# The first 512 sigmoid-gate columns of a decoder block, from four whole projections to seven half-sized products with three weight sums kept in HBM

## The chip, the cores and the metric

One core of one Trainium2 chip runs the whole block. The metric is the device time of one execution in microseconds; three executions of the kernel before gave 772.45, 772.70 and 772.75 us, so its median is 772.7 us. All tensors are float32. The matrix engine takes every factor as two parts, a high part `h` (rounded) and a low part `l = t - h`, and forms `h*h + h*l + l*h`; so each weight tile that is loaded costs one copy on the scalar engine and one subtraction on the vector engine before it can be used, and each product costs three matmuls where one would do.

Engine names below are those of the profile: PE (matrix engine), PEld (its weight loads), DVE (vector), ACT (scalar), POOL, SP (issues most DMAs).

## What is computed

One layer (DEPTH = 1) on 512 tokens of width 1024, cut to what this change touches:

```python
h = rms_norm(x, norm_mix)                       # 512 x 1024
proj = h @ w_in                                 # w_in: 1024 x 4400
u, q, kc, vc, ksl, vsl, kwn, vwn, g_nsa, g_merge = split(proj)
y_pool = pool_mixer(u, w_pool, pool_scale)      # 512 x 512
y_nsa  = nsa_mixer(q, kc, vc, ...)              # 512 x 1024, 16 heads, three branches
g_a, g_b = split(sigmoid(g_merge))              # 2 x 1024 columns
merged = g_a * (y_pool @ w_proj_pool) + g_b * (y_nsa @ w_proj_nsa)
x = x + merged @ w_out
x = x + square(relu(rms_norm(x) @ w_ff1)) @ w_ff2
return rms_norm(x, norm_final)
```

The change concerns `g_a`: 1024 columns of `w_in` (columns 2352 to 3375), in two groups of 512, here called group 0 and group 1.

## The kernel before

**Stages.** The program runs in four stretches on one core: a first stretch of projections out of `h` (in the profile about 11 to 166 us), attention with the remaining projections as filler between its small matmuls (to about 376 us), the output projections (to about 453 us), and the MLP. The first stretch is written as one list of keys, `P1`; each key is a weight tile and a piece of PE work. `ck`, `cv`, `ks`, `kw` are key and value projections, `u0` to `u3` the pooling inputs, `q0` to `q2` the first query pairs, `wk*` and `wv*` the first layer of the compression MLP for keys and values, `V0` to `V2` the value projection in three slices of the contraction, `wpool` and `PO0` to `PO3` the pooling mixer's output matmuls, `pp*` the pool projection. `ga0` to `ga3` are the four 128-column tiles of gate group 0.

**A projection** (`fm`, line 683; `mms`, line 519) is 24 matmuls of 512 columns (8 slices of the contraction, three part products each) into one PSUM bank.

**A half-sized group** (`class Group`, `product`, line 589). Gate group 1 is already formed with seven products instead of eight (Strassen's scheme in Winograd's form). The weights of a group, 1024 x 512, are cut into quarters `A11`, `A12`, `A21`, `A22`, each 512 x 256; `h` is cut into quarters 11, 12, 21, 22 (half the contraction by half the tokens). `S1` to `S4` are sums of weight quarters (`S1 = A21+A22`, `S3 = A11+A21`, `S2 = S1+A11`, `S4 = A12+S2`; signs are kept on the other side), `T1` to `T4` sums and differences of the quarters of `h`. The products are `A11*11`, `S3*T3`, `S1*T1`, `S2*T2`, `A12*21`, `A22*T4`, `S4*22`; each is 24 matmuls of 256 columns. They fill four PSUM banks: a (`A11`, then `A12` on top), b (`S2`), c (`S3`, then `A22` on top), d (`S1`, then `S4` on top). Before a bank is added to, DVE has to have read what stood in it: `main` copies a on ACT, and DVE forms `u2 = a - b`, `u3 = c + u2`, `u3 = d + u3` (lines 610, 611, 614); `last` forms the remaining results (line 624) and ACT applies the sigmoid (line 1123). So `A22`'s matmuls wait both for `T4` and for DVE's read of bank c.

**The token sums** `T1` to `T4` (`token_sums`, lines 1088 to 1107) are made once, on DVE and ACT, out of `h`. `T4` lies where the compression MLP for values keeps its intermediate results, so its two halves (ACT line 1104, DVE line 1107) come after that MLP's last small matmul (line 992), which in turn needs transposes (line 964), an ACT copy (`cg`, line 967) and the four `wv` matmuls (line 930).

**Loads and splits.** SP issues the weight loads in list order (`emit_load`, line 277) into four buffers `raw`; a load can be issued when the buffer it takes has been split. The split writes `wh`/`wl`, two pairs of buffers in turn (line 475 ACT and 478 DVE in halves; line 405 ACT and 407 DVE whole, for gate quarters), or the one pair `wkt`, used by `wk*`, `wv*` and by the products `S1` and `A22`. Sums of quarters of gate group 1 are formed in the `raw` buffers by DVE (line 403).

**Sums in HBM.** For the output projection and the MLP, sums of weight quarters are made without any engine's arithmetic: SP copies one quarter from HBM to HBM (`make_sum`, line 311) and, when that has landed, POOL adds the other quarter with an accumulating DMA (`add_sum`, line 319). `jobs` is the list of these sums; `sums_after(i)` says after which load one is begun, `begun` holds those whose addition is still to be issued. A copy whose source is itself such a sum waits on SP for the addition.

**Order.** Every engine runs its instructions in the order in which the program lists them. A small scheduler sets that order from the order of emission (generators in `side`, stepped once per piece of PE work) and a few marks of priority.

Of the kernel before, what the change touches and what calls it, by code (L numbers as in the profile page):

```python
# [62 lines left out]
def trunk(ctx: ExitStack, tc: tile.TileContext, A, out):  # L63
# [54 lines left out]
    def add_key(k):  # L118
# [14 lines left out]
        else:  # L133
# [1 line left out]
            add_cols(k, w_in, c0 + 128 * i)  # L135

    IN_COLS = {"ck": 1536, "cv": 1664, "ks": 1792, "kw": 2048}
    P1 = ("ck ks u0 wk0 u1 wk1 u2 wk2 kw wk3 cv V0 V1 V2 wv0 "
          "u3 wv1 q0 wv2 wpool ga0 PO0 ga1 q1 PO1 wv3 ga2 ga3 A11G1 PO2 S3G1 S1G1 S2G1 PO3 A12G1 "
          "A22G1 S4G1 q2 pp0 pp1 pp2 pp3").split()  # L140
    FILL2 = "gb0 q3 q4 q5 gb1 gb2 q6 gb3 q7 gb4 gb5 gb6 gb7".split()
    IN_TURN = ("A11", "S3", "S1", "S2", "A12", "A22", "S4")
    gate_loads = {}

    def add_gates(g):

        at = {b: len(LD) + n for n, b in enumerate(("21", "11", "22", "12"))}
        for b in at:
            i, j, c = int(b[0]) - 1, int(b[1]) - 1, 2352 + 512 * g
            w = w_in[512 * j:512 * j + 512, c + 256 * i:c + 256 * i + 256]  # L150
            LD.append([(w.rearrange("(k p) c -> p k c", p=128), 0)])
        gate_loads[g] = at

    for k in P1 + FILL2:
        if k[-2] == "G":
            if k[:3] == "A11":
                add_gates(int(k[-1]))
            WL.append((k, None))
        elif k[:2] != "PO":
            add_key(k)  # L160
        if k == P1[-1]:
            N1 = len(LD)
# [4 lines left out]
    WO_LATE = {"A22": 2, "S4": 3}  # L167
    WO_TURN = ("A11", "S1", "S3", "S2", "A12", "A22", "S4")
    wo_at = {}
    dp = ctx.enter_context(tc.tile_pool(name="sums", bufs=1, space=bass.MemoryType.DRAM))  # L170
    jobs, late, later = [], [], []
    wo_of = {f"A{i + 1}{j + 1}": w_o[512 * j:512 * j + 512, 256 * i:256 * i + 256].rearrange("(k p) c -> p k c", p=128)
             for i in range(2) for j in range(2)}
    for o, x, y in (("S1", "A21", "A22"), ("S3", "A11", "A21"), ("S2", "S1", "A11")):
# [83 lines left out]
    def emit_load():  # L258

        i = st["load"]  # L260
        if i >= len(LD):
            return False
        segs = LD[i]
        a = segs[0][0].shape[1]
        b = sum(s.shape[2] for s, _ in segs)
        assert a * b <= 1024
        if not by_name() or st["kept"] < RAW:
            st["kept"] += by_name()
            t = wp.tile([128, 1024], F32, tag="raw", bufs=RAW, name=f"raw{i}")
        elif spare:  # L270
            t = spare.pop(0)
        else:
            return False
        st["load"] += 1
        v = t[:, :a * b].rearrange("p (a b) -> p a b", a=a)
        for s, o in segs:
            began[0] = nc.sync.dma_start(v[:, :, o:o + s.shape[2]], s)
        raws[i] = (t, a, b)
        for _ in range(sums_after(i)):
            make_sum(began[0])  # L280
        if (26 <= i < N1 and len(begun) > 1) or i >= N1 + len(FILL2) + 4 and (len(begun) > 2 or begun and st["sums"] == len(jobs)):
            add_sum()
        while i == MLP0 + 6 and len(begun) > 2:
            add_sum()
        return True

    def sums_after(i):

        if i < MLP0:
            return 26 <= i < N1 and i % 2 == 0 or N1 + 3 <= i < N1 + len(FILL2) or i == MLP0 - 2  # L290
        if i < MLP0 + 12:
            return {3: 1, 6: 4}.get(i - MLP0, 0)
        return i % 3 == 0
# [35 lines left out]
    def slot_of(i):  # L329

        return shifted(slot_tiles(i), WL[i][0])
# [50 lines left out]
            held[to] = t  # L382

    kept = {}

    def gate_steps(i):

        o, g = WL[i][0][:-2], int(WL[i][0][-1])
        if o == "A11":
            kept.clear()  # L390
        for b in {"A11": ("11",), "S3": ("21",), "S1": ("22",), "A12": ("12",)}.get(o, ()):
            while st["load"] <= gate_loads[g][b]:
                assert emit_load()
# [1631 lines left out]
```

## Time and profile before

| | |
|---|---|
| median of three executions | 772.7 us |
| the profiled execution: its time, its span from first to last instruction | 773.65 us, 771.9 us |
| TensorE clock granted | 0.997 |
| busy: PE, PEld, DVE, ACT, POOL | 759.2, 674.9, 657.6, 507.9, 179.5 us |
| first stretch, 28.20 to 166.20 us: PE busy | 137.76 of 138.00 us |
| HBM read, written | 140.97 MB, 51.38 MB |

The profiled execution's span is 1.75 us under its own time, and its time 0.95 us over the median. Matmuls overlap: the profile gives one 512-column matmul a mean of some 0.39 us, but 24 of them follow each other in about 5.46 us; what a stretch of matmuls costs is read from start to start. A busy PE in this profile can hide waits of a tenth of a microsecond.

### The profile page before, as it was taken

The page shows a single profiled execution, that of the slowest core. Times are in us where ns is not written, and L with a number is a line of the kernel's source. Part 1 is how long each engine was busy: PE and PEld are TensorE (multiplying, and loading weights), DVE is VectorE, ACT ScalarE, POOL GpSimd, SP SyncE. Part 2 cuts the span into 40 slices and gives each one's busy share as a digit, 9 for nine tenths or more (in the row PEclk, how much of TensorE's full clock was granted, in tenths as well). Part 3 has the DMA queues.
Part 4 walks back from the last instruction along what each step waited for, and adds up shares of the span by engine and source line. Part 5 has one row for each costly group of instructions (what it writes and reads, how often), then busy time and mean ns, then how long its engine had stood idle before and what let it go on. Part 6 is the DMA issues. An engine that isn't in the chain of part 4 may idle for free.

```text
span 771.9 us, 13216 instructions
## 1 busy us (share of the span) xinstructions
PE 759.2 (98%) x4675; PEld 674.9 (87%) x4675; DVE 657.6 (85%) x1267; ACT 507.9 (66%) x977; POOL 179.5 (23%) x261
## 2 busy tenths in 40 slices
PE   8999999999999999999999999999999999999996
PEld 6889889888888888888889899989998899889985
DVE  6899868467988989989689679997899789978997
ACT  6668546247978888899645566953774477447754
POOL 4000011116646766574000110101111111111101
PEclk9999999999999999999999999999999999999998
DMA  9554875984051923281357975989997999899952
GB/s 304 144 146 121 231 170 156 213 217 124 15 147 56 183 55 70 48 144 48 120 180 222 327 117 177 288 210 269 320 279 209 301 316 250 229 316 296 279 189 109
DMA packets 117708, 146.55 MB, mean 190 GB/s; under 512 B 5653, under 2 KB 90169, under 8 KB 117434
## 3 DMA queue, kind: packets, MB, share of 16 engines
q1 hardware_dynamic: 97658, 120.28, 47.8%
q0 software_dynamic: 19696, 24.64, 21.4%
q10 hardware_dynamic: 288, 0.79, 0.3%
q8 instruction: 37, 0.61, 0.3%
q14 instruction: 29, 0.24, 0.1%
HBM read 140.97 MB, written 51.38 MB: 249 GB/s over the span
## 4 chain that ended last, share of the span: by engine, by line
PE 86%; DVE 8%; ACT 3%; issue 2%; POOL 0%; DMA 0%; DVEq 0%; ACTq 0%; POOLq 0%
PE psF L519 21%; PE psB L589 20%; PE psB L1639 15%; PE psB L519 6%; PE psS L1318 4%; PE psT L1380 4%; PE psO L1414 3%; PE psB L1587 3%; PE psV L589 3%; PE psV L519 2%; PE psF L651 1%; PE psC L930 1%; ACT P L1350 1%; DVE PT L1396 1%; DVE P L1340 1%
## 5 line engine op out<-in xcount | busy, mean ns | idle before, releaser
L519 PE MATMUL psF<-R,wh 128*128 128x512 f32 x448 | 144.4, 399 | 0.0
L319 POOL DMA_DIRECT2D S<-w_ff x44 | 49.1, 1116 | 358.2 <-DMA S<-w_ff 299.9
L366 ACT ACTIVATE wh<-raw 128x1024 fp32r<-128x1024 f32 x73 | 77.1, 1057 | 69.7 <-PE psB L589 27.3
L371 DVE TENSOR_TENSOR wl<-raw,wh 128x1024 fp32r<-128x1024 f32 x73 | 88.9, 1220 | 15.9 <-ACT wh L366 15.7
L1363 POOL TENSOR_SCALAR P<-P,sm,GT 128x128 f32<-128x128 f32 (+3 forms) x128 | 85.2, 716 | 68.1 <-DVE sm L1360 35.7
L519 PEld LDWEIGHTS psF<-R,wh 128*128 128x128 f32 x448 | 80.5, 188 | 13.6
L519 PE MATMUL psF<-R,wl 128*128 128x512 f32 x224 | 88.1, 394 | 0.0
L475 ACT ACTIVATE wh<-raw 128x512 fp32r<-128x512 f32 (+1 forms) x84 | 50.2, 618 | 48.7 <-PE psF L519 23.5
L1350 ACT ACTIVATE P<-P,sm 128x128 f32<-128x128 f32 (+3 forms) x128 | 71.0, 557 | 9.8 <-DVE sm L1340 6.2
L478 DVE TENSOR_TENSOR wl<-raw,wh 128x512 fp32r<-128x512 f32 (+1 forms) x82 | 57.0, 704 | 20.5 <-ACT wh L475 20.3
L1340 DVE CUSTOM_DVE_ANT_0 P<-psS,cst 128x128 f32<-128x128 f32 (+3 forms) x128 | 59.4, 483 | 5.0 <-PE psT L1380 3.2
L366 ACT ACTIVATE w3h<-raw 128x1024 fp32r<-128x1024 f32 x37 | 39.1, 1058 | 36.1 <-PE psB L589 11.0
L589 PE MATMUL psB<-R,wh 128*128 128x256 f32 x336 | 60.1, 280 | 0.0
L1396 DVE TENSOR_TENSOR PT<-psT,PT 128x512 fp32r<-128x512 f32 (+2 forms) x96 | 56.3, 592 | 2.3 <-ACT PT L1391 2.0
L1391 ACT ACTIVATE PT<-psT 128x512 fp32r<-128x512 f32 (+2 forms) x96 | 49.0, 520 | 11.9 <-PE psT L1380 11.0
L589 PEld LDWEIGHTS psB<-R,wh 128*128 128x128 f32 x336 | 51.5, 188 | 0.2
L1380 PE MATMUL psT<-ident,P 128*128 128x128 f32 x320 | 50.3, 273 | 0.9 <-DVE PT L1396 0.5
L371 DVE TENSOR_TENSOR w3l<-raw,w3h 128x1024 fp32r<-128x1024 f32 x37 | 45.1, 1220 | 5.7 <-ACT w3h L366 5.6
L519 PEld LDWEIGHTS psF<-R,wl 128*128 128x128 f32 x224 | 42.1, 188 | 8.7
L1414 PE MATMUL psO<-PT,VV 128*128 128x256 f32 x320 | 48.6, 287 | 0.0
L1380 PEld LDWEIGHTS psT<-ident,P 128*128 128x128 f32 x320 | 39.5, 140 | 10.2 <-issue 1.4
L589 PE MATMUL psB<-R,wl 128*128 128x256 f32 x168 | 46.9, 279 | 0.0
(430 smaller groups left out, 2157.6 us busy)
## 6 DMA issues: line engine op xcount, KB each, us to landing
raw<-w_ff SPq DMA_DIRECT2D x54, 512.0 KB, 6.0
S<-w_ff POOLq DMA_DIRECT2D x44, 512.0 KB, 8.7
raw<-S SPq DMA_DIRECT2D x44, 512.0 KB, 6.4
raw<-w_in SPq DMA_DIRECT2D x32, 512.0 KB, 4.3
S<-w_ff SPq DMA_DIRECT2D x32, 512.0 KB, 6.5
S<-S SPq DMA_DIRECT2D x12, 512.0 KB, 7.1
raw<-w_proj_nsa SPq DMA_DIRECT2D x8, 512.0 KB, 4.1
x<-x SPq DMA_DIRECT2D x7, 512.0 KB, 5.4
```

The lines of the kernel that those rows point to most:

```text
L366: ACT.activation(h, t, AF.Copy)
L371: DVE.tensor_tensor(l, t, h.bitcast(F32), op=ALU.subtract)
L478: eng.tensor_tensor(l[:, sl], t[:, sl], h[:, sl].bitcast(F32), op=ALU.subtract)
L519: PE.matmul(ps, a, b, start=first and j == 0, stop=last and j == n - 1, skip_group_check=True)
L589: PE.matmul(out, w[u][:, k, 128 * f:128 * f + 128], moving[v][:, k, :], **kw)
L1340: DVE.tensor_tensor_reduce(out=P[:, o:o + n].rearrange("p (a c) -> p a c", c=128), in0=s, in1=m, scale=1.0, scalar=3e38, op0=ALU.add, op1= ...
L1350: last_exp[:] = [ACT.activation(c, c, AF.Exp, bias=sm[:, 0, e:e + 1], scale=-1.0, accum_out=sm[:, 1, e:e + 1])]
L1363: r = POOL.tensor_scalar(P[:, o:o + n], P[:, o:o + n], sm[:, 2, e:e + 1], GT[:, qb, c + e:c + e + 1], op0=ALU.mult, op1=ALU.mult)
L1380: PE.transpose(pt[:, 128 * j:128 * j + 128], P[:, 128 * j:128 * j + 128], ident)
L1396: return DVE.tensor_tensor(dL, src, dH.bitcast(F32), op=ALU.subtract)
L1414: PE.matmul(ps[:, qb % 2, :, :], VV[:, k, b, g, :], t[:, j, :, :], start=False, stop=last and j == len(kbs) - 1 and t is tL, skip_group_ch ...
L1639: PE.matmul(ps[f], self.Y.of(y)[u][:, 2 * g + k, 128 * f:128 * f + 128], w[v][:, k, :], start=first and g == k == u == v == 0, stop=g == k ...
```

## The change

Gate group 0 (`ga0` to `ga3`) is formed by the same seven half-sized products as group 1. In difference to group 1, its sums `S1`, `S3` and `S2` are not added on DVE but made in HBM, by three more jobs at the head of the list `jobs`, begun after loads 8, 10 and 12 (`SUM0`); their additions are issued by POOL after loads 9, 11 and 13. Its three plain quarters `A11`, `A12`, `A22` and its three sums are then loaded like any weight; `S4 = A12 + S2` is still added on DVE. The list `P1` has another order: group 0's products take the place of `ga0` to `ga3`, `wv3` comes after `A11`, and `q2` is moved from behind group 1 to between the two groups. What follows in the program (attention, output projection, MLP) has the same instructions in the same order on PE, ACT and DVE; the sums for the MLP stand one place earlier against the loads.

```diff
-          "u3 wv1 q0 wv2 wpool ga0 PO0 ga1 q1 PO1 wv3 ga2 ga3 A11G1 PO2 S3G1 S1G1 S2G1 PO3 A12G1 "
-          "A22G1 S4G1 q2 pp0 pp1 pp2 pp3").split()
+    P1 = ("ck ks u0 wk0 u1 wk1 u2 wk2 kw wk3 cv V0 V1 V2 wv0 u3 wv1 q0 wv2 wpool A11G0 PO0 wv3 S3G0 PO1 S1G0 S2G0 PO2 q1 A12G0 A22G0 S4G0 PO3 q2 A11G1 S3G1 S1G1 S2G1 A12G1 A22G1 S4G1 pp0 pp1 pp2 pp3").split()
...
+    def sum_gates(g):
+        of = {}
+        for b in ("21", "11", "22", "12"):
+            i, j, c = int(b[0]) - 1, int(b[1]) - 1, 2352 + 512 * g
+            w = w_in[512 * j:512 * j + 512, c + 256 * i:c + 256 * i + 256]
+            of["A" + b] = w.rearrange("(k p) c -> p k c", p=128)
+        for o, x, y in (("S1", "A21", "A22"), ("S3", "A11", "A21"), ("S2", "S1", "A11")):
+            of[o] = dp.tile([128, 4, 256], F32, name=f"{o}_g{g}")
+            jobs.append((of[o], of[x], of[y]))
+        gate_of[g] = of
+
+    gate_of, gate_at = {}, {}
+    sum_gates(0)
...
+            g, o = int(k[-1]), k[:-2]
+            if g in gate_of:
+                if o in gate_of[g]:
+                    gate_at[k] = len(LD)
+                    LD.append([(gate_of[g][o], 0)])
+            elif o == "A11":
+                add_gates(g)
...
+        if i < 26 and begun and i % 2:
+            add_sum()
...
+    SUM0 = (8, 10, 12)
+
     def sums_after(i):
         if i < MLP0:
-            return 26 <= i < N1 and i % 2 == 0 or N1 + 3 <= i < N1 + len(FILL2) or i == MLP0 - 2
+            return i in SUM0 or 26 <= i < N1 and i % 2 == 0 or N1 + 3 <= i < N1 + len(FILL2) or i == MLP0 - 2
...
+        key = WL[i][0]
+        if g in gate_of:
+            if o in gate_of[g]:
+                while st["load"] <= gate_at[key]:
+                    assert emit_load()
+                kept[o] = raws.pop(gate_at[key])[0]
+            h, l = dest[key][:2] if key in dest else slot_of(i)
+            t = kept.pop("A12" if o == "S4" else o)
+            ACT.activation(h, t, AF.Copy)
+            yield
+            with tc.high_priority(60) if o in ("S1",) else nullcontext():
+                DVE.tensor_tensor(l, t, h.bitcast(F32), op=ALU.subtract)
+            hls[i] = tuple(x.rearrange("p (a b) -> p a b", a=4) for x in (h, l))
+            if o == "A12":
+                yield
+                (POOL if GP else DVE).tensor_tensor(t, t, kept["S2"], op=ALU.add)
...
```

In the changed file the same instructions carry other line numbers: the load is line 298, the copy in HBM 336, its addition on POOL 344, a projection's matmul 568, a half-sized product's 638, a split of group 0 429 (ACT) and 432 (DVE), `S4`'s sum 436, `u2`, `u3`, `u3` 659, 660, 663, the token sums' halves 1153 and 1156, the pooling output 1116.

How the instructions move is shown at two places. First SP's queue, in the stretch in which the keys `kw` to `wv0` are loaded. Before:

```order
L277 DMA raw_464<-w_in 128x8x128
L277 DMA raw_494<-w_ck 128x4x256
L277 DMA raw_517<-w_in 128x8x128
L277 DMA raw_554<-w_in 128x3x128
L277 DMA raw_554<-w_in 128x3x176
L277 DMA raw_580<-w_in 128x3x128
L277 DMA raw_580<-w_in 128x3x176
L277 DMA raw_621<-w_in 128x2x128
L277 DMA raw_621<-w_in 128x2x176
L277 DMA raw_644<-w_cv 128x4x256
L819 DMA rs<-rx 32x512 x4
```

Now (`S_g_70`, `S_g_71`, `S_g_72` are `S1`, `S3`, `S2` of group 0 in HBM; `raw_560`, `raw_587`, `raw_629` are `V0`, `V1`, `V2`; `raw_653` is `wv0`):

```order
L336 DMA S_g_70<-w_in 512x1x256
L298 DMA raw_498<-w_ck 128x4x256
L298 DMA raw_522<-w_in 128x8x128
L336 DMA S_g_71<-w_in 512x1x256
L298 DMA raw_560<-w_in 128x3x128
L298 DMA raw_560<-w_in 128x3x176
L298 DMA raw_587<-w_in 128x3x128
L298 DMA raw_587<-w_in 128x3x176
L336 DMA S_g_72<-S_g_70 16x8192
L298 DMA raw_629<-w_in 128x2x128
L298 DMA raw_629<-w_in 128x2x176
L298 DMA raw_653<-w_cv 128x4x256
```

Three copies of 512 KB stand between the loads, the third behind the addition into `S_g_70` and ahead of `V2` and `wv0`. POOL's queue, empty in this stretch before, has the three additions.

Second, DVE's queue up to the low half of `T4` (`TS<-MA,TS`). Before, in gate group 1, between the splits of `S2` and `A22`:

```order
L407 TENSOR_TENSOR wl_1340<-raw_1134,wh_1339 128x1024
L1067 SCALAR_TENSOR_TENSOR yd_370<-psF,pec,yd_369 128x512
L407 TENSOR_TENSOR wl_1406<-raw_1214,wh_1405 128x1024
L403 TENSOR_TENSOR raw_1214<-raw_1214,raw_1134 128x1024
L998 CAST VC_137<-psM 32x64
L1107 TENSOR_TENSOR TS<-MA,TS 128x1024
L999 TENSOR_TENSOR VC_137<-psM,VC_137 32x64
L998 CAST VC_138<-psM 32x64
L407 TENSOR_TENSOR wkt_364<-raw_1156,wkt_363 128x1024
```

Now, in gate group 0, from the sum for `S4` on:

```order
L436 TENSOR_TENSOR raw_1070<-raw_1070,raw_1021 128x1024
L663 TENSOR_TENSOR gs<-psV,gs 128x512
L432 TENSOR_TENSOR wkt_367<-raw_1106,wkt_366 128x1024
L432 TENSOR_TENSOR wl_1296<-raw_1070,wh_1295 128x1024
L1047 CAST VC_140<-psM 32x64
L1048 TENSOR_TENSOR VC_140<-psM,VC_140 32x64
L1047 CAST VC_141<-psM 32x64
L1048 TENSOR_TENSOR VC_141<-psM,VC_141 32x64
L1047 CAST VC_142<-psM 32x64
L1156 TENSOR_TENSOR TS<-MA,TS 128x1024
```

`T4`'s low half has moved ahead by one gate group, and within its group it has moved back: it stood ahead of the splits of `A22` (`wkt`) and `S4` and behind one of the eight small operations of the value compression (`VC`), and stands now behind both splits and five of the eight.

More of the change, by code (lines that the diff above doesn't have):

```diff
@@ L137, in trunk @@
     IN_COLS = {"ck": 1536, "cv": 1664, "ks": 1792, "kw": 2048}
-    P1 = ("ck ks u0 wk0 u1 wk1 u2 wk2 kw wk3 cv V0 V1 V2 wv0 "
-          "u3 wv1 q0 wv2 wpool ga0 PO0 ga1 q1 PO1 wv3 ga2 ga3 A11G1 PO2 S3G1 S1G1 S2G1 PO3 A12G1 "
-          "A22G1 S4G1 q2 pp0 pp1 pp2 pp3").split()
+    P1 = ("ck ks u0 wk0 u1 wk1 u2 wk2 kw wk3 cv V0 V1 V2 wv0 u3 wv1 q0 wv2 wpool A11G0 PO0 wv3 S3G0 PO1 S1G0 S2G0 PO2 q1 A12G0 A22G0 S4G0 PO3 q2 A11G1 S3G1 S1G1 S2G1 A12G1 A22G1 S4G1 pp0 pp1 pp2 pp3").split()
     FILL2 = "gb0 q3 q4 q5 gb1 gb2 q6 gb3 q7 gb4 gb5 gb6 gb7".split()
@@ L143, in trunk @@
     gate_loads = {}
+    dp = ctx.enter_context(tc.tile_pool(name="sums", bufs=1, space=bass.MemoryType.DRAM))
+    jobs = []
     def add_gates(g):
-        at = {b: len(LD) + n for n, b in enumerate(("21", "11", "22", "12"))}
-        for b in at:
+        of = {}
+        for b in ("21", "11", "22", "12"):
             i, j, c = int(b[0]) - 1, int(b[1]) - 1, 2352 + 512 * g
             w = w_in[512 * j:512 * j + 512, c + 256 * i:c + 256 * i + 256]
-            LD.append([(w.rearrange("(k p) c -> p k c", p=128), 0)])
-        gate_loads[g] = at
+            of["A" + b] = w.rearrange("(k p) c -> p k c", p=128)
+        gate_loads[g] = {b: len(LD) + n for n, b in enumerate(("21", "11", "22", "12"))}
+        for b in ("21", "11", "22", "12"):
+            LD.append([(of["A" + b], 0)])
+    def sum_gates(g):
+        of = {}
+        for b in ("21", "11", "22", "12"):
+            i, j, c = int(b[0]) - 1, int(b[1]) - 1, 2352 + 512 * g
+            w = w_in[512 * j:512 * j + 512, c + 256 * i:c + 256 * i + 256]
+            of["A" + b] = w.rearrange("(k p) c -> p k c", p=128)
+        for o, x, y in (("S1", "A21", "A22"), ("S3", "A11", "A21"), ("S2", "S1", "A11")):
[4 more added lines that the diff above has]
+    sum_gates(0)
+    EARLY = len(jobs)
     for k in P1 + FILL2:
         if k[-2] == "G":
-            if k[:3] == "A11":
-                add_gates(int(k[-1]))
+            g, o = int(k[-1]), k[:-2]
[5 more added lines that the diff above has]
+                add_gates(g)
             WL.append((k, None))
@@ L169, in trunk @@
     wo_at = {}
-    dp = ctx.enter_context(tc.tile_pool(name="sums", bufs=1, space=bass.MemoryType.DRAM))
-    jobs, late, later = [], [], []
+    late, later = [], []
     wo_of = {f"A{i + 1}{j + 1}": w_o[512 * j:512 * j + 512, 256 * i:256 * i + 256].rearrange("(k p) c -> p k c", p=128)
@@ L384, in trunk @@
     kept = {}
+    GP = False
     def gate_steps(i):
@@ L390, in gate_steps @@
             kept.clear()
-        for b in {"A11": ("11",), "S3": ("21",), "S1": ("22",), "A12": ("12",)}.get(o, ()):
+        for b in () if g in gate_of else {"A11": ("11",), "S3": ("21",), "S1": ("22",), "A12": ("12",)}.get(o, ()):
             while st["load"] <= gate_loads[g][b]:
@@ L394, in gate_steps @@
             kept[b] = raws.pop(gate_loads[g][b])[0]
+        key = WL[i][0]
[14 more added lines that the diff above has]
+                (POOL if GP else DVE).tensor_tensor(t, t, kept["S2"], op=ALU.add)
+            if o in ("A12", "S2"):
+                kept[o] = t
+                if o == "S2":
+                    return
+                kept.pop("S2")
+            emit_load()
+            return
         h, l = dest[WL[i][0]][:2] if WL[i][0] in dest else slot_of(i)
```

## Prediction

> **What bounds the kernel now.** I read the page first, then the chain of waits in order of time, then PE's waits and the busy time of the first stretch.
>
> ```profile
> PE 759.2 (98%) x4675; PEld 674.9 (87%) x4675; DVE 657.6 (85%) x1267; ACT 507.9 (66%) x977; POOL 179.5 (23%) x261
> ...
> 28.20:166.20 138.00, 137.76 (x761) 120.19 (x761) 110.36 (x199) 73.75 (x131) 9.02 (x11) 1.00 0.69 175
> ...
> PE psC L930 <- DVE cA L914: 0.2, 1, 0.2
> ```
>
> The second line is a stretch with the busy time of PE, PEld, DVE, ACT and POOL (instructions in brackets), then clock, DMA share and GB/s. PE is busy for 137.76 of 138.00 us in the stretch that is changed, and the third line is its only wait there. So what is taken from PE here comes off the end, as long as PE does not begin to wait; DVE, at 110.36 us, is the engine to watch. The chain gives PE's own pace:
>
> ```profile
> 85.73 6.15 PE psF L519 x27
> 92.23 11.80 PE psF L519 x51
> 104.62 10.95 PE psF L519 x48
> 115.57 2.80 PE psV L589 x24
> 119.07 3.53 PE psV L589 x30
> 122.86 1.62 PE psV L589 x12
> 124.85 3.71 PE psV L589 x30
> 129.26 8.40 PE psV L589 x72
> 137.66 28.59 PE psF L519 x126
> ```
>
> (start, length, what, how many). A projection's 24 matmuls take 10.95 / 2 = 5.47 us, 0.228 us each, a half-sized product's 24 take 2.80 us, 0.117 us each. The third to fifth `L589` rows have two interludes of the value compression in them, 129.26 - 119.07 - 3 x 2.80 - 0.69 (the three `PO3` matmuls) = 1.1 us.
>
> **The saving.** Out go four projections, 4 x 5.47 = 21.9 us; in come seven half-sized products, 7 x 2.80 = 19.6 us. PE gains 2.2 us, 0.29% of the whole. No other matmul is added or dropped; the interludes and `PO` only move. That is the most the change can bring.
>
> The Trainium skill ("TensorE: Matmul & The Clock Gate", section "Back-to-back issue gap") gives a sustained 131 ns a matmul at 512 columns and 81 ns at 128, weight loads included, and would speak against half-sized products. By it the 96 matmuls that go cost 12.6 us and the 168 that come at least 13.6 us, so PE would lose 1 us or more. The rows above contradict it for this kernel, 228 against 117 ns, and the measurement decides.
>
> **The added work on the side.** The rows that price it, DVE and ACT:
>
> ```profile
> L371 DVE TENSOR_TENSOR wl<-raw,wh 128x1024 fp32r<-128x1024 f32 x73 | 88.9, 1220 | 15.9 <-ACT wh L366 15.7
> L366 ACT ACTIVATE wh<-raw 128x1024 fp32r<-128x1024 f32 x73 | 77.1, 1057 | 69.7 <-PE psB L589 27.3 <-PE psB L1639 18.1 <-DVE raw L355 8.6
> ...
> 76.21 2.35 DVE L1107 TENSOR_TENSOR TS<-MA,TS 128x1024 fp32r<-128x1024 f32 x2
> ...
> 91.10 0.42 DVE L836 TENSOR_TENSOR rs<-rs,cst 128x256 f32<-128x256 f32 x1
> 91.44 0.42 DVE L836 TENSOR_TENSOR rx<-rx,cst 128x256 f32<-128x256 f32 x1
> ...
> 93.05 0.74 DVE L1067 SCALAR_TENSOR_TENSOR yd<-psF,pec,yd 128x512 fp32r<-128x512 f32 x1
> ...
> 127.13 0.20 DVE L999 TENSOR_TENSOR VC<-psM,VC 32x64 fp32r<-32x64 f32 x1
> 127.36 0.21 DVE L998 CAST VC<-psM 32x64 fp32r<-32x64 f32 x1
> ...
> 138.30 1.28 DVE L478 TENSOR_TENSOR wl<-raw,wh 128x512 fp32r<-128x512 f32 x2
> ...
> 85.73:143.11 57.38, 57.38 (x339) 50.61 (x339) 42.04 (x68) 28.47 (x45) 7.03 (x8) 1.00 0.77 190
> ```
>
> DVE's operations overlap a little: two of 1024 columns take 2.35 us, so the next can follow 1.15 us later, for 512 columns 0.60, for 256 columns 0.34, for the pooling output 0.67, for a `VC` operation 0.23. Group 0 puts seven splits and the sum for `S4` (8 x 1.22) and five operations on its banks (5 x 0.69) in the place of eight half splits (8 x 0.69): DVE has 13.2 - 5.5 = 7.7 us more to do. Between the start of `ga0` and the end of `q2` it stands idle for 57.38 - 42.04 = 15.3 us, so on the average it still fits. ACT gets about 3 us more and has 29 us free. The sum of a stage does not decide, though; four places do.
>
> *`T4` for `A22` of group 0.* The order shows that `T4`'s low half now comes at the end of a long run on DVE. PE arrives at `A22` after 85.73 + `A11` 2.80 + `PO0` 0.69 + `wv3` 0.94 + `S3` 2.80 + `PO1` 0.69 + `S1`, `S2` 5.60 + `PO2` 0.69 + `q1` 5.47 + `A12` 2.80 + interludes 1.1 = 109.3 us. DVE's run begins with `T2`'s low half, and this cannot begin before ACT has made the high one:
>
> ```profile
> 86.77 0.69 DVE L1035 TENSOR_TENSOR yd<-ea,yd 128x512 fp32r<-128x512 f32 x1
> ...
> 87.68 1.04 ACT L1104 ACTIVATE TS<-MA 128x1024 fp32r<-128x1024 f32 x1
> ...
> 124.89 1.06 ACT L1104 ACTIVATE TS<-MA 128x1024 fp32r<-128x1024 f32 x1 [1.71 <-PE psM L992]
> ```
>
> ACT's copy comes right behind the pooling mixer's last operation, as it does now (86.77, then 87.68). That operation stands behind four more DVE operations' worth of work than now (`S3`'s split whole instead of half, and half of `wv3`'s), some 1.5 us, so it ends near 88.9, the copy near 90.0. From there to `T4`'s low half DVE has to do, in its order: seven of 1024 columns (8.05), five of 512 (3.0), three pooling outputs (2.0), two for a query (1.4), ten of 256 columns for the rotation and the compression (3.4), one small one (0.2), five `VC` (1.15) and `T4`'s own (1.22): 20.4 us, so it ends at 110.4 if DVE never waits. It waits at one place that I can see: `S4`'s split needs ACT's copy, which stands behind a sigmoid that waits for DVE and needs the buffers that `q1` gives up at 105.4. I reckon that ACT is done at 107.6 where DVE is free at 107.1. With this and the wait of `VC` for the interlude, `T4` is ready at 111.1. `A22`'s second matmul needs it: PE waits 111.1 - 109.3 - 0.1 = **1.7 us**, between 1.0 (DVE never waits) and 2.4.
>
> *Bank c for `A22` of group 1.* `q2`'s rotation now falls into group 1. PE reaches the end of `A12` at about 136.9. DVE's six rotation operations wait for the four DMAs of swapped rows, which ACT, behind `S3`'s copy, lets go at 124.4; four issues (2.4 us) and a landing later it is 129.2. Then 6 x 0.34, the splits of `A12` and `A22`, two operations for the query, `u2`, `S4`'s sum and `u3`: 2.0 + 2.3 + 1.4 + 0.6 + 1.15 + 0.7 = 8.1 us, so bank c is read at 137.3 and PE waits **0.4 us** (0 to 1.2).
>
> ```profile
> 144.12 2.43 SPq L819 DMA_DIRECT2D rs<-rx  x4
> rs<-rx SPq DMA_DIRECT2D x8, 64.0 KB, 2.4
> ```
>
> *The three sums beside the loads of the value stage.* Rows of this stretch, then the queues' shares and the copy and addition in HBM:
>
> ```profile
> 51.75 0.37 SPq L277 DMA_DIRECT2D raw<-w_cv  x1
> 56.04 1.16 ACT L475 ACTIVATE wkt<-raw 128x512 fp32r<-128x512 f32 x2 [0.44 <-DMA raw<-w_cv]
> 57.22 10.90 PE psV L519 x78
> 65.40 0.85 DVE L478 TENSOR_TENSOR wl<-raw,wh 128x304 fp32r<-128x304 f32 x2
> ...
> 45.00:54.00 9.00, 9.00 (x47) 7.63 (x46) 8.79 (x17) 6.54 (x13) 0.00 (x0) 1.00 0.38 96
> ...
> q1 hardware_dynamic: 97658, 120.28, 47.8%
> q0 software_dynamic: 19696, 24.64, 21.4%
> ...
> S<-w_ff POOLq DMA_DIRECT2D x44, 512.0 KB, 8.7
> ...
> S<-w_ff SPq DMA_DIRECT2D x32, 512.0 KB, 6.5
> ...
> DMA to landing us min/median/max: 4.4/6.0/7.8
> ```
>
> `wv0` is loaded at 51.75, and ACT already waits for its landing at 56. Behind its split stand those of `V1` and `V2` on a DVE that is busy for 8.79 of 9 us; `V2`'s ends at 66.25, and PE takes `V2` up at 57.1 + 72 x 0.138 = 67.0. So `wv0` may come 0.65 us later for nothing, and each us beyond costs PE one. The first copy lands about 6.5 us after 31.5, its addition 8.7 us later, at 47; the third copy waits for that on SP, which would go on with `V2` only at 49.9, so SP loses nothing as long as this takes less than 2.9 us more. But the DMA engines fill up: 47.8% of 771.9 us for 120.28 MB are 3.1 us a MB for a copy, 21.4% for 24.64 MB 6.7 us for an addition; between 45 and 54 us one and a third additions and a copy (0.52 MB each) add 6.2 us to the 3.4 that are used of 9. The last line is the landing time of weight loads between 128 and 150 us, where two such additions and two copies run beside them: 4.4 to 7.8 us, against the 4.2 that `wv0` takes now. At the median that is 1.8 us more, in a milder case nothing; I take 1.05, so PE waits **0.4 us** (0 to 2.9).
>
> The skill's page "DMA: Bandwidth & Descriptors", section "Issuing engines are not separate DMA queues", says the same of the mechanism: a transfer that POOL issues runs on the same 16 engines as SP's. The landing times agree.
>
> *Small ones.* `wv3` now follows `A11` at once, and its split ends at 89.5 where PE starts on it at 89.2; `q1`'s first low half ends 0.1 us after its first use: together **0.2 us** (0 to 0.6). In attention POOL issues one addition more than before, 1.1 us on an engine with 23% of work: nothing (0 to 0.7). `S1`'s split through `wkt` after `wv3` has 0.1 us to spare, `S2`'s bank 0.9. The loads of the sums themselves come 13 us after the last addition.
>
> **The sum.** -2.2 + 1.7 + 0.4 + 0.4 + 0.2 = +0.5 us on the profiled span of 771.9, so 772.4 there, and 773.2 on the scale of the median, 772.7. The gain on PE is there, and DVE and the DMA engines give it back.
>
> **The rivals.** *The gain stays* (faster). If `T4` comes in time, or its wait hides the later ones, PE keeps most of 2.2 us: 772.7 - 2.2 + 0.6 = 771.1 us, down to 770.5. For it speaks that today's stretch runs without a wait at equally full engines, and that DVE has 15.3 us to spare; against it that DVE's run of 20.4 us starts 19.3 us before PE arrives, without any wait counted.
>
> *The sums hold up the value stage* (slower). One mechanism, `wv0`'s landing: from 2.1 us late on (after 58.0) the whole comes out over 0.2% slower; at the 7.8 us of the last row above it is 3.6 us late, PE waits 2.9, and the time is 773.2 - 0.4 + 2.9 = 775.7 us. For it: ACT already waits for this load, and the additions fall on it. Against: the queue is the emptiest of the stretch there (0.38).
>
> *A half product costs more than half.* If the matmuls of group 0 were paced by their weight loads at 188 ns instead, 168 x 0.071 = 12 us would come on top, 785 us. Group 1's 168 and the MLP's, all at 0.117, say no.
>
> ```profile
> L589 PEld LDWEIGHTS psB<-R,wh 128*128 128x128 f32 x336 | 51.5, 188 | 0.2
> ```
>
> By the skill's rule above, the one on the issue gap, it would be 1 us and the waits, about 776 us.
>
> That the sums are not used is out: the order shows the loads from `S_g` and seven products.
>
> **How the numbers follow.** This forecast 0.58, the gain stays 0.15, the sums hold up 0.25, the dear half product 0.02. A difference under 0.2% (1.5 us) can hardly be told from none. The forecast lies within it; of its own range, 771.7 to 774.7, a little is outside on each side. So faster 0.15, the same 0.59, slower 0.26. The range to 8 in 10 goes from 771.2 (the gain mostly kept) to 775.6 (`wv0` 3.5 us late).
>
> **What would show it.** In the profile after: PE's waits have a row for `psV` (the product line) waiting for DVE's `TS`, 1.0 to 2.4 us, at 109 to 112 us; a smaller one for DVE's `u3` some 27 us later; perhaps one of `psV` in the value stage at 67 us for DVE's `wl`, with ACT's wait for `raw<-w_cv` grown from 0.44 us. The pool projections start at 143 us, as now. Seven products without interludes take 19.6 us. I am wrong on the main step if `T4` is ready at PE's arrival, on the sums if `wv0` lands within 4.9 us, and on the frame if attention or the MLP, whose order is unchanged, moves by more than 0.7 us.

## The result, and the profile after

The changed kernel takes 780.2 us (median of six executions, 777.1 to 780.8), the kernel before 772.6 beside it (six, 772.3 to 773.0). The ratio is 1.0091, 95% interval 1.0074 to 1.0108: **slower by 0.9%**, 7.6 us, where 773.2 us and a range to 775.6 were forecast.

The profiled execution took 780.78 us, its span is 778.9 us, 7.0 more than the 771.9 of before. Read off the first matmul of each stretch in the two traces, in us:

| stretch | before | after | difference |
|---|---|---|---|
| start to the first `wk0` matmul | 31.4 | 30.1 | -1.3 |
| to the first matmul of `V0` | 25.7 | 25.7 | 0 |
| value stage: `V0` to the first of `wv0` | 14.8 | 19.0 | +4.2 |
| gate groups: `wv0` to the first pool projection | 71.1 | 74.0 | +2.9 |
| pool projection, attention, output projections, the MLP's beginning (to the first matmul on quarter 21 of its hidden values, at 510.3 us before and 516.2 after) | 367.4 | 367.4 | 0 |
| the rest of the MLP, to the end | 261.5 | 262.7 | +1.2 |

So the loss stands at three places, and two of them are not where the forecast had put a wait. PE's waits in the first 200 us of the changed kernel that the kernel before does not have (who waits, for whom, us in total, how often, the longest):

```profile
PE psV L638 <- ACT wh L454: 2.0, 1, 2.0
PE psV L568 <- DVE wl L527: 1.3, 3, 0.6
PE psM L1026 <- ACT cg L1016: 1.0, 1, 1.0
...
PE psV L638 <- DVE wl L456: 0.8, 1, 0.8
PE psV L568 <- ACT wh L524: 0.6, 1, 0.6
```

The second, third and fifth of these rows are the value stage, the first and fourth are `S3` of gate group 1. No row waits for `TS`: `T4` costs nothing.

**The value stage.** The load of `wv0` in the kernel before (who waited for its landing, how long; issue to landing):

```profile
  ACT wkt L475: 0.4, 1
...
DMA to landing us min/median/max: 4.2/4.2/4.2
```

The same after:

```profile
  ACT wkt L524: 4.7, 1
...
DMA to landing us min/median/max: 8.4/8.4/8.4
```

And DVE in the changed kernel from there on (start, length, line, operation, and in brackets how long it stood idle for whom):

```profile
59.69 0.69 DVE L527 TENSOR_TENSOR wkt<-raw,wkt 128x512 fp32r<-128x512 f32 x1 [4.15 <-ACT wkt L524]
...
61.23 0.41 DVE L885 TENSOR_TENSOR rx<-rx,cst 128x256 f32<-128x256 f32 x1
61.57 0.41 DVE L999 SCALAR_TENSOR_TENSOR ea<-ea 64x256 f32<-64x256 f32 x1
61.90 0.46 DVE L527 TENSOR_TENSOR wl<-raw,wh 128x304 fp32r<-128x304 f32 x1
```

`wv0` lands at 58.94 us in the place of 55.96. Its split stands on ACT and DVE ahead of the rotation and of `V1`'s split (the last row), so both engines idle for it for over 4 us. (The rotation mixes each row of a key or a query with a swapped row; four small DMAs fetch the swapped rows, `rs<-rx`, and DVE's operations on `rx` and `rs` wait for them.) The same operations follow each other in both kernels down to the compression's small copy `cg`, for which PE waits; ACT makes it at 69.57 us before and at 72.55 after:

```profile
69.57 0.28 ACT L967 ACTIVATE cg<-psM 128x128 f32<-128x128 f32 x1
...
72.55 0.28 ACT L1016 ACTIVATE cg<-psM 128x128 f32<-128x128 f32 x1
```

The DMA engines are busier in this stretch. Before (the last three columns are the clock, the DMA share and GB/s):

```profile
31.00:62.00 31.00, 30.76 (x165) 26.82 (x165) 30.61 (x62) 20.54 (x37) 0.16 (x1) 1.00 0.57 156
```

and after:

```profile
31.00:62.00 31.00, 30.39 (x160) 26.10 (x158) 26.46 (x55) 16.76 (x31) 3.66 (x3) 1.00 0.94 236
```

**Gate group 1.** DVE around the rotation rows of `q1` in the changed kernel:

```profile
115.33 0.69 DVE L527 TENSOR_TENSOR wl<-raw,wh 128x512 fp32r<-128x512 f32 x1
119.82 0.43 DVE L885 TENSOR_TENSOR rx<-rx,cst 128x256 f32<-128x256 f32 x1 [3.80 <-DMA rs<-rx]
...
126.70 2.47 DVE L452 TENSOR_TENSOR raw<-raw,raw 128x1024 f32<-128x1024 f32 x2
```

PE at the products of `S3`:

```profile
129.42 0.50 PE L638 MATMUL psV<-TS,wh 128*128 128x256 f32 x2 [1.96 <-ACT wh L454]
130.68 0.58 PE L638 MATMUL psV<-TS,wl 128*128 128x256 f32 x1 [0.76 <-DVE wl L456]
```

DVE stands 3.8 us for the four DMAs with the swapped rows of `q1`; `S3`'s sum (L452) is behind, and PE, with `A11` done, waits 2.0 and 0.8 us. Then the granted clock falls (the third column from the end):

```profile
124.00:127.40 3.40, 3.28 (x26) 2.89 (x24) 3.30 (x5) 1.06 (x2) 1.17 (x1) 1.00 0.99 152
127.40:130.20 2.80, 0.56 (x3) 0.30 (x2) 2.54 (x3) 1.89 (x3) 0.00 (x0) 0.99 1.04 140
130.20:133.60 3.40, 2.92 (x13) 2.92 (x14) 3.37 (x4) 2.14 (x3) 0.00 (x0) 0.50 0.55 116
133.60:137.00 3.40, 3.40 (x31) 3.40 (x30) 3.40 (x8) 1.70 (x3) 0.00 (x0) 1.00 0.46 154
```

**The MLP.** PE's one wait in the rest of the MLP:

```profile
PE psB L1688 <- ACT wh L391: 1.4, 1, 1.4
```

POOL and ACT in order of time around it:

```profile
524.98 1.16 POOL L344 DMA_DIRECT2D S<-w_ff  x1 [9.88 <-DMA S<-w_ff]
...
534.71 1.06 ACT L391 ACTIVATE w3h<-raw 128x1024 fp32r<-128x1024 f32 x1 [4.01 <-DMA raw<-w_ff]
```

An addition of the MLP's sums is issued at 524.98, a load on SP at 525.49; the load lands after 9.1 us. In the kernel before the same load (519.61) lands after 5.1 us; one addition is issued 5.0 us ahead of it (514.63) and the next 6.9 us behind it:

```profile
526.55 1.16 POOL L319 DMA_DIRECT2D S<-w_ff  x1 [10.77 <-DMA S<-w_ff]
```

### The profile page after: what moved, and what is told of

The parts are those of the page before. It is cut to its first block, busy times and chain, and to the rows that moved or that the text cites. A ratio compares the mean times of both kernels' runs of the same rounds, so it can differ in the third digit from the quotient of the medians.

```text
span 778.9 us, 13388 instructions
## 1 busy us (share of the span) xinstructions
PE 759.9 (98%) x4747; PEld 676.9 (87%) x4747; DVE 664.7 (85%) x1272; ACT 510.4 (66%) x977; POOL 182.8 (23%) x264
## 4 chain that ended last, share of the span: by engine, by line
PE 73%; DVE 13%; ACT 5%; DMA 4%; issue 3%; POOL 1%; SPq 0%; DVEq 0%; ACTq 0%; POOLq 0%
PE psB L638 18%; PE psF L568 16%; PE psB L1688 10%; PE psB L568 6%; PE psV L638 4%; PE psS L1367 4%; PE psT L1429 4%; PE psO L1463 3%; PE psB L1636 3%; DVE wl L396 1%; PE psF L700 1%; DMA raw<-w_in 1%; DMA raw<-w_ff 1%; DMA rs<-rx 1%; DVE wl L527 1%
## 5 line engine op out<-in xcount | busy, mean ns | idle before, releaser
L568 PE MATMUL psF<-R,wh 128*128 128x512 f32 x384 | 124.5, 400 | 0.0
L396 DVE TENSOR_TENSOR wl<-raw,wh 128x1024 fp32r<-128x1024 f32 x73 | 88.9, 1220 | 15.7 <-ACT wh L391 12.1
L568 PEld LDWEIGHTS psF<-R,wh 128*128 128x128 f32 x384 | 68.7, 188 | 11.3
L568 PE MATMUL psF<-R,wl 128*128 128x512 f32 x192 | 75.6, 394 | 0.0
L524 ACT ACTIVATE wh<-raw 128x512 fp32r<-128x512 f32 (+1 forms) x76 | 44.8, 616 | 39.0 <-PE psF L568 23.8
L391 ACT ACTIVATE w3h<-raw 128x1024 fp32r<-128x1024 f32 x37 | 39.1, 1058 | 37.9 <-PE psB L638 14.8
L527 DVE TENSOR_TENSOR wl<-raw,wh 128x512 fp32r<-128x512 f32 (+1 forms) x74 | 51.4, 707 | 9.5 <-ACT wh L524 9.2
L1463 PEld LDWEIGHTS psO<-PT,VV 128*128 128x128 f32 x320 | 42.2, 188 | 1.4 <-ACT PT L1440 0.3
```

The source lines that it names most:

```text
L527: eng.tensor_tensor(l[:, sl], t[:, sl], h[:, sl].bitcast(F32), op=ALU.subtract)
L568: PE.matmul(ps, a, b, start=first and j == 0, stop=last and j == n - 1, skip_group_check=True)
L1463: PE.matmul(ps[:, qb % 2, :, :], VV[:, k, b, g, :], t[:, j, :, :], start=False, stop=last and j == len(kbs) - 1 and t is tL, skip_group_ch ...
```

## The experiments

Theories: A, the sums of group 0 hold up the value stage; B, sums of the later stages beside `q1`'s rows hold up group 1; C, the MLP's sums begin at another place. (Where the expectations say 37 us into the MLP, they count from some 499 us of the changed kernel, and their 261 us for the MLP are the last row of the table above.) The executions of most of these kernels lie further apart (up to 6 us) than those of the kernel before (2 to 3 us), so a stage is read from the profile and a time from the median.

**The sums alone** (the kernel before, with three sums that nobody reads).

```diff
+    sum_gates(0)
...
+    SUM0 = (8, 10, 12)
...
+        if i < 26 and begun and i % 2:
+            add_sum()
...
-            return 26 <= i < N1 and i % 2 == 0 or ...
+            return i in SUM0 or 26 <= i < N1 and i % 2 == 0 or ...
```

> The kernel before, with the three sums of gate group 0 made in HBM at the same three loads as in the change, and nobody reading them: the four whole projections stay. Theory A (the sums' transfers hold up the rotation rows and the loads of the value stage): the stretch from the first wk0 matmul to the first wv0 matmul grows from 40.6 us to about 44.8 as in the change, the swapped rows of kw land some 7 us after their issue in the place of 3 to 4, and the time is 776 to 777 us. Rival (the loss there belongs to the new order of the keys, not to the transfers): the stretch stays at 40.6 us and the time at 772.6.

Measured 775.9 us (773.7 to 779.5), ratio 1.0039 (1.0023 to 1.0055). The profiled execution is the slowest, 779.5: its value stage takes 21.2 us, `wv0` lands at 62.0, PE waits 2.8 us,

```profile
PE psV L538 <- ACT wh L494: 2.8, 1, 2.8
```

and then runs at half clock (windows of this kernel; the clock is the third column from the end):

```profile
61.80:64.00 2.20, 0.05 (x1) 0.00 (x0) 1.25 (x3) 1.35 (x3) 0.00 (x0) 1.00 0.09 28
64.00:70.80 6.80, 5.70 (x19) 4.99 (x20) 6.77 (x14) 4.58 (x10) 0.00 (x0) 0.50 0.62 156
70.80:74.00 3.20, 3.20 (x24) 3.15 (x23) 2.76 (x5) 3.03 (x6) 0.00 (x0) 1.00 0.23 30
```

The gate groups take 71.2 us, as before. A holds: without any new order of the keys the transfers alone cost 2.8 us in the median. The stretch from `wk0` to `wv0` is 46.9 us in this slow execution, where 44.8 was expected.

**The later sums moved away from `q1`'s rows.**

```diff
-            return i in SUM0 or 26 <= i < N1 and i % 2 == 0 or ...
+            return SUM0.count(i) or i in (26, 33, 35, 36, 39) or ...
```

> The change, with four of the sums of the output projection and the MLP begun later (after loads 26, 33, 35, 36 and 39 in the place of every second load from 26 to 36), so that no copy and no addition runs while the swapped rows of q1 are on their way. Theory B (the rows of q1 land late behind these transfers, DVE stands behind them, and S3 of group 1 comes late): the rows land within 3 us of their issue, DVE's idle time of 3.8 us ahead of the rotation goes, PE's waits of 2.0 and 0.8 us for S3 of group 1 go, the granted clock there stays at 1.00, the stretch from A11 of group 0 to the first pool projection is 55.2 to 55.8 us in the place of 60.3, and the time falls by 4.5 to 5 us to about 775.5; by 1.4 more if the wait in the MLP comes from the one sum more and goes too. Rival (DVE has too much to do there, with or without these transfers): the waits stay over 1.5 us and the time within 1.5 us of the change. The value stage is as in the change (44.8 us) by both.

Measured 775.0 us (773.2 to 777.6), 5.2 under the change. PE's only wait from 80 to 170 us:

```profile
PE psV L638 <- DVE gs L660: 0.2, 1, 0.2
```

DVE at the rows of `q1`:

```profile
113.65 0.69 DVE L527 TENSOR_TENSOR wl<-raw,wh 128x512 fp32r<-128x512 f32 x1
114.26 0.51 DVE L885 TENSOR_TENSOR rx<-rx,cst 128x256 f32<-128x256 f32 x1
```

The window around them, here

```profile
114.00:120.00 6.00, 6.00 (x38) 5.34 (x37) 5.80 (x12) 3.55 (x6) 0.49 (x1) 1.00 0.44 137
```

and in the change:

```profile
114.00:120.00 6.00, 6.00 (x44) 5.66 (x43) 2.08 (x6) 1.14 (x2) 1.09 (x2) 1.00 1.04 272
```

DVE goes on at once, the DMA share falls from 1.04 to 0.44, the clock stays at 1.00, and the gate groups take 69.8 us, 1.3 under the kernel before: B holds, and the rival of a DVE with too much work falls. (The rows land after 3.8 us in the median, not within the 3 that were expected, and that is in time.) The value stage took 16.0 us in this execution and not 19.0 as in the change's, with the same three sums at the same loads: its loss differs between executions. PE's wait in the MLP is still there, 0.9 us.

**Group 0's sums earlier, and both moves.**

```diff
-    SUM0 = (8, 10, 12)
+    SUM0 = (5, 5, 8)
```

> The change, with the three sums of group 0 begun earlier: two copies after load 5 (at some 17 us, where the DMA engines are nearly idle until 25) and the third after load 8, in the place of loads 8, 10 and 12. Theory A: the transfers are over before the value stage, its stretch goes back to 40.6 to 41.5 us, and the time falls by 3 to 4 us to about 776.5; group 1's waits stay as in the change. Rival (the additions only move the harm: the loads of the key stage and the first rotation rows come late): a wait of 1 us or more appears on PE between 25 and 50 us and less than 2 us is won.

> Both moves at once. By theories A and B together the losses of 4.2 and 4.9 us go and what stays is the saving on PE of 2.2 us less small waits: 770.5 to 772 us, that is at or under the kernel before. If either is wrong, its share stays: 776 without B, 775 without A.

The first: 777.4 us (775.8 to 778.5). The value stage takes 15.9 us, `wv0` lands after 4.7, no wait appears in the key stage, and DVE's 3.75 us behind `q1`'s rows and PE's 2.0 and 0.8 are unchanged, so A and B are separate. The time is 2.8 us under the change, a little short of the 3 to 4 expected. Both moves: 772.7 us (771.2 to 776.7), ratio 1.0005 (0.9988 to 1.0021); the stages are 15.7 and 70.0 us. That is the 7.5 us back, and no gain that can be measured; 770.5 to 772 was expected.

**No sums in HBM.** Group 0's quarters are loaded like group 1's and added in the load buffers, `wv3` ahead of `A11`, later sums after loads 24, 31, 33, 34, 37; added by POOL for group 0, by POOL for both groups, by DVE.

```diff
-    sum_gates(0)
...
-            DVE.tensor_tensor(t, t, kept[b], op=ALU.add)
+            (POOL if g == 0 else DVE).tensor_tensor(t, t, kept[b], op=ALU.add)
```

> Group 0 by seven half-sized products without any sum in HBM: its four weight quarters are loaded as those of group 1 are, S3, S1, S2 and S4 are added by POOL (idle there) in the load buffers, wv3 stands ahead of A11, and the later sums begin as in the run before this one (after loads 24, 31, 33, 34, 37). Theory (what is lost is lost to the transfers of the sums, PE's 2.2 us are real): the value stage has its 40.6 us with no wait over 0.3 us, no wait of 2 us for S3 of group 1, and the time is 770.5 to 771.5 us, 1 to 2 us under the kernel before, with a spread between executions no wider than the kernel before has (2 us). Rival (the sums are needed early and POOL or DVE is too slow for them): PE waits for S3, S1 or S2 of group 0 for 1.5 us or more together and the time is 772.5 or more.

> As the run before, with the sums of group 1 on POOL too. If DVE paces the groups, this takes 4.9 us off DVE and is 0.3 to 1 us faster than the run before; if a sum's own length paces them (POOL should take about 2.5 us for 1024 columns by its 1.25 us for 512, DVE 1.2), S3 and S1 of group 1 come later and it is 0.5 to 2 us slower.

> As the first of these, with all the sums on DVE: 3.7 us more for it than in the change, in the stretch in which it is busiest. Theory: PE waits 1 to 3 us in all for splits of group 0 and the time is 772 to 774 us. Rival (DVE has room enough there): as the first within 0.3 us.

Measured 778.4, 785.4 and 774.6 us (ratios 1.0073, 1.0160, 1.0022). The theory's figure for the first was missed by 7 us, and not because a sum came late: DVE stands while POOL adds, 2.4 to 2.8 us each time here (POOL, then DVE, in the first of the three):

```profile
84.41 5.22 POOL L451 TENSOR_TENSOR raw<-raw,raw 128x1024 f32<-128x1024 f32 x2 [53.42 <-DMA raw<-w_in]
...
84.96 2.25 DVE L1080 TENSOR_TENSOR ea<-ea,cst 128x16 f32<-128x16 f32 x1
87.24 0.17 DVE L1081 TENSOR_TENSOR ea<-ea,ea 128x16 f32<-128x16 f32 x1
87.35 2.83 DVE L526 TENSOR_TENSOR wkt<-raw,wkt 128x512 fp32r<-128x512 f32 x1
```

and PE behind it:

```profile
PE psC L978 <- DVE wkt L526: 3.3, 1, 3.3
```

An operation of 16 columns takes 2.25 us, beside 0.17 for its like; a split of 0.69 takes 2.83. The 3.3 us are PE's wait for that split (of `wv3`, not of a sum), and behind it the clock is at one half for 3.4 us. With the sums of both groups on POOL the price doubles. With DVE it is 0.6 us over the expected range, 1.3 us of waits and a stretch at half clock behind them.

**Group 0's sums behind the value stage, and both moves once more.** The first has `SUM0 = (16, 17, 19)` with the later sums moved, the second is the kernel with both moves again (the early sums and the later sums moved).

> The change with the later sums moved as before, and the three sums of group 0 begun after loads 16, 17 and 19, that is behind the rotation rows and the loads of the value stage, from 58 us on, where the DMA engines are half free until 85. Theory A: the value stage is as in the kernel before (no wait over 0.5 us but for the start's own), the sums are there when S3, S1 and S2 are loaded at 79 to 86 us, and the time is 771.2 to 772.2 us, with fewer executions over 774 than with the early sums, since less stands in the way of the key stage's loads. Rival (the sums come too late, or hold up the loads of wv2, wv3 and A11): PE waits 1 us or more for S2 or for wv3 between 85 and 100 us, and the time is 773 or more.

> The kernel with both moves once more, beside the run before this one, for a second profile and an interval: 771.5 to 773 us in the median; if the profiled execution is one of those over 775, it shows where the late DMA then falls.

774.3 us (771.9 to 775.2; ratio 1.0008, 0.9997 to 1.0018) and 773.8 us (772.5 to 776.8; ratio 1.0006). In the first PE waits 1.2 us for `wv3`'s split at 91 us, so the rival is right. The second is over the 771.5 to 773 us that were expected; its profile has the MLP's wait of 1.6 us again, at the same load.

**The MLP's order of DMAs.** In the MLP a sum is begun after every third load, counted from the start of the list. The change has two loads more ahead of it (six for group 0 in the place of four), so the same rule falls on other loads: the copy that stood behind the 94th load of the kernel before stands behind the 95th of the same loads now, and so on through the MLP, a load later each time. In the change, and with the early sums alone, one sum more is also begun before attention, so that each single sum begins two loads earlier; with the later sums moved it begins one later. (The expectation's "a load earlier" fits neither.)

```diff
-        return i % 3 == 0
+        return i % 3 == 2
```

With it SP's order of the MLP's loads and of all later copies is that of the kernel before. In the first run beside both moves, in the second alone (with one sum fewer before attention, so that their number is as before).

> The kernel with both moves, and a third: a sum in the MLP is begun after every load whose number leaves the remainder 2 by three, in the place of 0. The change has two loads more ahead of the MLP, so that by the old rule the same sums begin a load earlier there; now SP's queue in the MLP is as in the kernel before. Theory C (an addition that is issued 0.5 us ahead of a load makes it land 4 to 5 us late, which is the wait of 0.9 to 1.6 us some 37 us into the MLP): that wait is gone in every execution, the MLP takes 261 to 261.5 us, and the time is 771.5 to 772.3 us, 0.1 to 0.2% under the kernel before, with less spread. Rival (that wait is chance and may fall in either order): as the runs before, 772.7 to 773.8 us.

> The change with the MLP's sums back in their old places against the loads (and one sum fewer ahead of attention, so that their number is as before), and nothing else: by theory C the wait in the MLP of 1.4 us goes and the others stay, 778 to 779 us, against 780.2; the value stage and group 1 as in the change.

Measured 773.6 us (772.5 to 775.8; ratio 1.0004, 0.9995 to 1.0014) and 778.7 us (four executions, 778.1 to 781.6; ratio 1.0081, 1.0063 to 1.0099). The rest of the MLP takes 261.0 and 260.9 us, with no such wait in either. Of the six profiles with the moved order three have it (1.4, 0.9, 1.6 us at the same place), of those with the old order (the kernel before, the sums alone, the three without sums in HBM, these two) none. That fits C. So does the distance: in the three with the wait the addition is issued 0.50 to 0.57 us ahead of the load, which lands after 8.7 to 9.4 us; in the other three of the moved order 0.65 to 1.0 us ahead, and the load lands after 5.3 to 6.8; in the old order some 5 us ahead. In these six profiles, then, a tenth of a microsecond separates the two; why, no run here shows. The second run's median is 1.5 us under the change as expected, but the two intervals overlap (the change: 1.0074 to 1.0108), and the first is not faster than its like. So C's share of the time between executions is not shown, and the spread has another cause as well.

**The split of `wv0` behind that of `V2`.** In eleven of the thirteen profiles so far the value stage ends 15.8 to 15.9 us after `wv0`'s landing (before 55.96 and 71.81, after 58.94 and 74.77, the sums alone 62.00 and 77.89, both moves 56.07 and 71.88). The two others have 16.1 and 16.3.

```diff
-                conv[0] = ACT.activation(h[:, sl], t[:, sl], AF.Copy)
+                with behind(v2[0]) if WL[i][0] == "wv0" else nullcontext():
+                    conv[0] = ACT.activation(h[:, sl], t[:, sl], AF.Copy)
+                if WL[i][0] == "V2":
+                    v2[:] = conv
```

> The kernel with the three moves, and the split of wv0 issued on ACT behind that of V2 (on DVE it follows). Theory D: the stage no longer ends 15.8 us after wv0's landing but when PE is through, 14.8 to 15.0 us after its first matmul, PE's wait for the compression's small matmul (0.5 to 1.0 us) goes, and the time is 0.5 to 1 us under the run of the three moves: 772 to 772.8 us beside 773.3 for the kernel before. Rival: the rows of the rotation, which land right behind wv0, or ACT and DVE's own work hold the stage at the same end within 0.3 us, and the time is 773.3 to 773.8.

> The kernel before with the split of wv0 behind that of V2, and nothing else. PE had no wait in its value stage, so the time stays at 773 to 773.4 us by both theories in the median; by D its executions with an earlier start or a later wv0 gain, 0.2 to 0.4 us.

With the three moves (early sums, later sums moved, the MLP's old order) it takes 772.4 us (771.8 to 776.4; ratio 0.9991, 0.9981 to 1.0001), the fastest of all and 0.85 us under the kernel before; its interval still includes a ratio of 1. The time is the one that theory D expected. The kernel before with this alone: 773.4 us, ratio 1.0004 (0.9995 to 1.0013). But theory D falls in its form, and the time is no proof of it: the stage takes 15.9 us, and PE's wait stays:

```profile
PE psM L1030 <- ACT cg L1020: 0.9, 1, 0.9
```

ACT ahead of it (the first row is the moved split):

```profile
64.66 1.14 ACT L526 ACTIVATE wkt<-raw 128x512 fp32r<-128x512 f32 x2
...
68.61 1.15 ACT L526 ACTIVATE wh<-raw 128x512 fp32r<-128x512 f32 x2
69.78 0.28 ACT L1020 ACTIVATE cg<-psM 128x128 f32<-128x128 f32 x1
```

ACT comes to the compression's small copy (`cg`) at 69.8 us by its own work, the moved split now among it: from 62.64 us on it never stands for more than 0.14 us. So in this profile, with `wv0` on time, DVE's and ACT's work from the rotation rows on sets the stage's end, and an earlier start of PE would gain nothing there.

## Why the prediction was wrong, point by point

Three steps of the sum failed. PE's wait for `T4` was priced at 1.7 us and is nothing; `wv0`'s landing was priced at 5.25 us and took 8.4; `q1`'s rotation rows were priced at nothing and cost about 4 us. A fourth loss, 1.2 us in the MLP, lay outside the frame. The 1.7 us for `T4`, which did not come, hide a part of what the other terms lacked.

- **The saving, -2.2 us: the mechanism stands.** With the transfers out of the way the gate groups take 69.8 to 70.0 us against 71.1, 1.1 to 1.3 us less, with bank c's 0.5 us (below) in it; the rest to 2.2 is some ten pieces that each last 0.03 to 0.1 us longer than reckoned.
- **`T4`, +1.7 us: fell.** DVE's side was right: the low half was to be ready 25.4 us after `A11`'s start (111.1 - 85.73), and ends at 113.96, 25.3 after 88.69. The step that failed is "`A22`'s second matmul needs it: PE waits". PE's own order has four matmuls of `S4` ahead of `A22`'s first and ten between its first and second, 14 x 0.117 = 1.64 us, nearly the whole wait. `T4` is ready 0.05 us before its use, so it costs nothing by a narrow margin (DVE's row for `T4`, then PE):

```profile
112.73 1.23 DVE L1156 TENSOR_TENSOR TS<-MA,TS 128x1024 fp32r<-128x1024 f32 x1
...
112.66 0.34 PE L638 MATMUL psV<-TS,wkt 128*128 128x256 f32 x1
112.84 0.28 PE L638 MATMUL psV<-R,wh 128*128 128x256 f32 x1
...
114.01 2.96 PE L638 MATMUL psV<-TS,wkt 128*128 128x256 f32 x23
```

- **Bank c, +0.4 us: right, and hidden in the change.** Where `S3` of group 1 is on time, `A12` lasts 3.25 to 3.3 us to the next product's first matmul in the place of 2.80, some 0.5 us, and the row of PE's wait is for DVE's `u3` (`gs`). In the change PE is late already.
- **The sums beside the value stage, +0.4 us (0 to 2.9): the mechanism was right, two terms mis-sized.** It is the rival "the sums hold up the value stage", `wv0`'s landing as it said. The landing took 8.4 us, not 5.25; and the slack of 0.65 us, reckoned to `V2`'s split (67.0 - 66.25 is 0.75; the other 0.1 has no row), was not there, since behind that split the chain goes on to `cg`, which is ready at 69.85 us in the kernel before and used at 70.09. All of the 2.98 us by which `wv0` is later in absolute time comes out at the stage's end (2.96). The other 1.26 of the 4.22 us is PE's earlier start, which is lost there.
- **Small ones, +0.2 us:** no such wait in the change.
- **Group 1, not in the forecast, about +4 us** (waits of 2.0 and 0.8, and 1.3 for the clock below). The landing of rotation rows was priced at 2.4 us for `q2` and nothing for `q1`, although `q1`'s stand between loads and sums on SP. They took 6.0 us in the median:

```profile
  DVE rx L885: 3.8, 1
...
DMA to landing us min/median/max: 4.4/6.0/6.1
```

- **The clock, not in the forecast.** The terms took PE's pace at full clock behind a wait; 3.4 us at half clock made `S3` about 1.3 us longer (5.25 us against 3.95 behind the same waits at full clock, with the early sums alone moved).
- **"Attention or the MLP, whose order is unchanged":** true of PE, ACT and DVE, not of SP. The change of place was seen (the front's "one place earlier"; counted in loads, each sum begins two earlier and the copies stand one later), and costed on POOL alone (0 to 0.7). It put an addition just ahead of a load: a wait of 1.4 us, +1.2 us on the stretch. That the wait comes of this order is likely by the profiles above, not shown by the times.

The sum in place of +0.5: 7.0 us on the span, -1.3 for the start (which differs between executions, 29.8 to 31.4 us in these profiles), +4.2, +2.9, +1.2.

## What to carry to other kernels

A sum in HBM takes hardly any engine's time (1.16 us of POOL to issue an addition), but its transfers can delay what shares the DMA engines with them; look not for the sum's own deadline but for the small transfers and the loads behind which an in-order engine stands, and put the sums where none of these is on its way. When a list of loads grows, every rule that counts from its start moves work in stages that nobody touched, so compare the DMA queues there as well. And a wait is only priced when the waiting engine's own order has been read up to the instruction that needs the data.

## What the runs showed of the hardware

**The clock after a short wait.** Waits of 2.0 and 0.8 us with 0.5 us of matmuls between them halved the granted clock for 3.4 us in the change, 2.8 us of waiting for 6.8 us in the run with the sums alone; the same 2.0 and 0.8 us with group 0's sums earlier left it at 1.00:

```profile
124.80:127.50 2.70, 0.51 (x3) 0.30 (x2) 2.44 (x3) 1.84 (x3) 0.00 (x0) 1.00 1.01 134
127.50:131.00 3.50, 2.97 (x25) 2.98 (x26) 3.47 (x4) 2.34 (x4) 0.00 (x0) 1.00 0.56 116
```

In the run with all the sums on DVE even waits of 0.3, 0.2 and 0.8 us within 3 us did so, for 3.4 us. So a wait is paid a second time in some profiles and not in others. The Trainium skill ("TensorE: Matmul & The Clock Gate", section "What's actually happening") tells of a monitor whose windows of about 3.4 us run freely, not with the kernel. The lengths of 3.4 and 6.8 us and the difference between the profiles agree with that. By the rule in its section "HAM oscillation — how this bites in real kernels", PE is to have no idle gap over some 3.4 us; to keep to that was not enough here, gaps of 2.0 and 0.8 us halved the clock.

**POOL stops DVE, but not every operation.** While POOL adds one tile of 1024 columns to another (2.4 to 3.3 us), a DVE operation with both inputs in SBUF that begins in that time does not end before POOL has: it lasts up to 2.1 us longer, whatever its own size (2.25 us in the place of 0.17, 2.83 in the place of 0.69). The value compression's small operations, which read PSUM (`psM`), go on at their usual length beside it (POOL, then DVE, in the same run):

```profile
111.12 2.39 POOL L451 TENSOR_TENSOR raw<-raw,raw 128x1024 f32<-128x1024 f32 x1 [12.69 <-DVE wl L455]
...
111.72 0.21 DVE L1047 TENSOR_TENSOR VC<-psM,VC 32x64 fp32r<-32x64 f32 x1
...
112.70 1.90 DVE L1155 TENSOR_TENSOR TS<-MA,TS 128x1024 fp32r<-128x1024 f32 x1
```

The Trainium skill ("Advanced Engine Details and Errata", section "Mode Summary") says that GpSimd, which is POOL, shares VectorE's second port and that the two block each other in VectorE's two-port modes. The trace shows a stop of the same kind; no run here tells which port it is, or that DVE was in such a mode.
